# Asking for the half-heads 2 and 3 of the linear attention at four steps per product instead of two

## The chip, the cores and the metric

The kernel runs on one core of a Trainium2 chip. The metric is the time of one launch on the device, in microseconds. Beside the times there is a profile of one execution, which shows what each engine did when. TensorE is called PE in it, VectorE DVE, ScalarE ACT, GpSimd POOL, and SyncE, which issues most DMAs, SP.

## The reference

The kernel computes two layers of a streaming-encoder trunk on 512 tokens of width 2048, in float32. Each layer normalises its input, projects it to 7184 columns, and splits them between a gated linear attention (GLA, four heads, called half-heads here since they make one half of the output's input) and a chunked attention of eight heads. Each group is normalised per head, gated and concatenated; one output projection, a second normalisation and the residual follow.

```python
z = h @ w_in
gq, gk, gv, gg, ga, aq, ak, av, ag = split_columns(z)
...
U = jnp.einsum('bnchk,bnchv->bnhkv', k_dec, vf)
...
new = a[..., None] * state + u
...
o = jnp.einsum('bnchk,bnhkv->bnchv', qf, states)
...
o_gla = rmsnorm(o_gla, g_gla.reshape(GLA_HEADS, GLA_DV)).reshape(B, S, D_GLA)
o_gla = o_gla * jax.nn.silu(gg)
...
y = jnp.concatenate([o_gla, o_att], axis=-1) @ w_out
return x + rmsnorm(y, g_post)
```

The recurrence goes over eight chunks of 64 tokens: U is the outer product of a chunk's decayed keys and its values, the state is decayed and U added, and the chunk's queries read the new state.

## The kernel before

The projections are done in blocks of 512 columns. Float32 products are made of three matmuls on a high and a low part of each operand: `wh` is the weight's rounded copy (ACT, L203), `wl` the rest (DVE, L207). Some blocks are plain (`std_gemm`, matmuls at L323): for each of eight 256-row chunks of the contraction, four token tiles with six matmuls each. Others go in pairs (`fast_gemm`, L409 and L399) with a Strassen-like scheme of seven products (P1, P5, P6, P3, P7, P2, P4) of four chunks each; one chunk of a product is twelve matmuls of 128x512. A list called `stream` fixes the order of all weight blocks, and `ahead` loads and splits them a few entries in advance.

Between these matmuls the small work of the two attentions is woven in. It is written as Python generators in a list `tasks`; one advance of the first generator is a step. After each matmul group `Pace` calls `pump` with so many steps as its `rate` says; `delayed` holds work that comes due a number of steps later. The finished program is then put in order by the framework's scheduler, which places each engine's instructions by what it reckons to be ready.

The last pair of a layer's input blocks is the value pair, `PAIRS[5]`. Its products P3 and P7 finish the values of half-heads 2 and 3 (`j` = 1 in `gv_consume`), and P2 and P4 those of half-heads 0 and 1. When the second token half of a `j` is there, `gv_consume` appends `gla_heads(j, ...)` to `tasks`: for `j` = 1 alone, for `j` = 0 beside `early_sums`, of which one step is taken for every third of the heads. `gla_heads` works on four units, one for each half-head and each token half p. A unit's steps are:

- `outer` (PE, L1060): twelve matmuls with 64 contraction rows, two groups of six that go to the two PSUM tiles `ps_u[0]` and `ps_u[1]`, for even and odd chunks.
- `states` (SP loads the gate, L1069; DVE, L1079 and L1081): four dependent updates of the state.
- `read` (PE, L1094): four matmuls that read the states into `ps_o`.
- `norm` (ACT, L1104 and L451; POOL's power, L447).
- `gate` (DVE, L1112), which leaves the gated output in a buffer `bias` or `sg`, used in turn.
- `turn`, five steps later (PE transposes, L1122; ACT, L1133; POOL stores it, L1137; ACT and DVE split it, L108 and L109), which makes an operand of the output projection.

The names `bias` and `sg` in L1122's rows are those buffers, `a120` to `a123` and `g4`, `g5`, `g16`, `g17` the operands that the turns make. The small PSUM tiles (`ax`) come from a pool of four buffers.

Next in `stream` is the first output block, `std_gemm(l, NB_IN, ...)` at a rate of 1.7 steps per six matmuls. Its chunks come in the order `OO`, the GLA half-heads last, in the order 2, 3, 0, 1. Behind it `until(lambda: len(og) == 8)` takes what steps the turns still need, the eight loads of x are issued on POOL behind the last norm (L479), and the second block begins with `NB_IN + 1` and two of four token tiles. `early_sums` and `output_sums` load the attention outputs back (SP, L637 for `fa`, L641 for `fg`), form sums and differences of them (DVE, L604, split by L108 and L109) and store them (POOL, L611), for the last pair of the output projection.

Of the kernel before, what the change touches and what calls it, by code (L numbers as in the profile page):

```python
# [34 lines left out]
def hybrid_trunk(  # L35
# [92 lines left out]
    PAIRS = ((GG0, GG1), (AV0, AV1), (QK01, QK23), (QK45, QK67), (GK, GQ), (GV0, GV1))  # L128
# [558 lines left out]
    def layer(l):  # L687
# [520 lines left out]
                tasks.append(heads if j else beside(heads, early_sums(), 3))  # L1208


        fast_gemm(l, PAIRS[5], gv_consume, rate=2, after=fetch_operands)
        A.clear()


# [113 lines left out]
    for l in range(L):  # L1328
        layer(l)
# [54 lines left out]
```

## Time and profile before

| what | value |
|---|---|
| median of three runs | 1643.76 us (1642.11 to 1644.25) |
| the profiled execution | 1642.16 us, span 1640.4 us |
| instructions | 24886 |
| busy PE, DVE, ACT, POOL | 1623.6, 1227.6, 905.5, 178.2 us |
| DMA, mean over the span | 286 GB/s |

The span is the time from the first to the last instruction; the execution's own time has 1.8 us more around it. A row of the timeline gives the start, the duration, the engine, the line and the operation, the tile written and those read, the shape, and the count of instructions that were merged; square brackets hold the idle time just before it and what ended that. Matmuls overlap, so the pitch of a stream of them is read from the difference of their starts. In a row of the waits stand the waiting engine and line, what it waited for, the total, the count and the longest.

### The profile page before, as it was taken

Reading aid. Unit: us, or ns where it says so; the run is one execution under the profiler, and the core shown is the slowest. Engines: PE = TensorE matmul, PEld = TensorE weight load, DVE = VectorE, ACT = ScalarE, POOL = GpSimd, SP = SyncE. Lnnn points to the kernel's source line nnn. Section 1 sums busy time; section 2 is a strip of 40 time slices with the busy share of each in tenths; the row PEclk is TensorE's granted clock in tenths of the full one; section 3 lists DMA queues with packets and bytes.
Section 4 is the critical chain, followed back from the end, with each engine's and each line's share of the span. In section 5 each row is a group of like instructions: output and inputs, shape, how many; then the busy total and the mean of one; then the engine's idle time right before and its main releaser. Section 6 shows DMA issues by size and latency. Waiting matters only on the chain.

```text
span 1640.4 us, 24886 instructions
## 1 busy us (share of the span) xinstructions
PE 1623.6 (99%) x9030; PEld 1392.1 (85%) x9030; DVE 1227.6 (75%) x1579; ACT 905.5 (55%) x1515; POOL 178.2 (11%) x259
## 2 busy tenths in 40 slices
PE   9999999999999999999999999999999999999997
PEld 7888889999988877688888888899999888776886
DVE  7567776877877876678776676768778778857887
ACT  7444544556666644455784445445556765445553
POOL 1210000001101201310132000000001001013111
PEclk9999999999999999999999999999999999999999
DMA  9979796958858696899779797968588676967996
GB/s 380 350 273 320 281 313 228 309 173 309 293 179 297 206 383 211 283 370 357 285 257 383 267 338 258 322 220 302 192 310 271 207 271 232 357 230 287 394 327 226
DMA packets 150490, 469.59 MB, mean 286 GB/s; under 512 B 16396, under 2 KB 35604, under 8 KB 150368
## 3 DMA queue, kind: packets, MB, share of 16 engines
q1 hardware_dynamic: 127632, 389.36, 68.3%
q0 software_dynamic: 22016, 77.37, 12.1%
q8 instruction: 71, 1.16, 0.3%
q10 hardware_dynamic: 720, 1.28, 0.2%
q14 instruction: 51, 0.42, 0.1%
HBM read 395.83 MB, written 71.06 MB: 285 GB/s over the span
## 4 chain that ended last, share of the span: by engine, by line
PE 97%; DVE 1%; DMA 1%; ACT 1%; issue 0%; DVEq 0%; POOL 0%; SPq 0%; ACTq 0%; POOLq 0%
PE mm L409 45%; PE mm L323 21%; PE mm L399 20%; PE ax L890 2%; PE ax L409 1%; PE ax L873 1%; PE ax L1060 1%; PE ax L721 1%; PE ax L1094 1%; PE ax L853 1%; PE ax L852 1%; PE ax L851 1%; DMA t<-fg 0%; PE ax L921 0%; PE ax L551 0%
## 5 line engine op out<-in xcount | busy, mean ns | idle before, releaser
L409 PE MATMUL mm<-wh,sa 128*128 128x512 f32 x1536 | 484.6, 391 | 0.1
L203 ACT CAST wh<-raw 128x1024 fp32r<-128x1024 f32 x256 | 270.1, 1056 | 262.9 <-PE mm L409 113.3
L207 DVE TENSOR_TENSOR wl<-raw,wh 128x1024 fp32r<-128x1024 f32 x256 | 312.6, 1222 | 122.6 <-PE mm L323 39.0
L203 ACT CAST wh<-H 128x1024 fp32r<-128x1024 f32 x224 | 235.5, 1053 | 221.4 <-PE mm L409 115.1
L207 DVE TENSOR_TENSOR wl<-H,wh 128x1024 fp32r<-128x1024 f32 x224 | 273.8, 1223 | 109.0 <-PE mm L409 50.4
L409 PEld LDWEIGHTS mm<-wh,sa 128*128 128x128 f32 x1536 | 288.0, 188 | 62.3 <-issue 2.4
L409 PE MATMUL mm<-wl,sa 128*128 128x512 f32 x768 | 300.3, 391 | 0.1
L399 PE MATMUL mm<-sa,wh 128*128 128x256 f32 x1280 | 237.1, 285 | 0.0
L399 PEld LDWEIGHTS mm<-sa,wh 128*128 128x128 f32 x1280 | 199.9, 191 | 0.3
L409 PE MATMUL mm<-wh,a 128*128 128x512 f32 x576 | 186.3, 393 | 0.0
L399 PE MATMUL mm<-sa,wl 128*128 128x256 f32 x640 | 180.6, 283 | 0.0
L323 PE MATMUL mm<-wh,a 128*128 128x512 f32 x512 | 167.9, 394 | 4.0 <-ACT a L108 1.2
L409 PEld LDWEIGHTS mm<-wl,sa 128*128 128x128 f32 x768 | 144.2, 188 | 29.6 <-DVE wl L207 0.5
L447 POOL TENSOR_TENSOR sm<-sm,mhalf 128x4 f32<-128x4 f32 (+2 forms) x40 | 67.1, 1678 | 767.1 <-DVE sm L906 542.0
L197 DVE TENSOR_TENSOR H<-H,raw 128x1024 f32<-128x1024 f32 x120 | 146.5, 1221 | 1.7
L409 PEld LDWEIGHTS mm<-wh,a 128*128 128x128 f32 x576 | 108.0, 188 | 22.5
L399 PEld LDWEIGHTS mm<-sa,wl 128*128 128x128 f32 x640 | 122.3, 191 | 0.1
L323 PEld LDWEIGHTS mm<-wh,a 128*128 128x128 f32 x512 | 96.0, 188 | 27.5 <-DVE g L1242 2.0
L409 PE MATMUL mm<-wl,a 128*128 128x512 f32 x288 | 112.9, 392 | 0.0
L323 PE MATMUL mm<-wl,a 128*128 128x512 f32 x256 | 100.4, 392 | 0.5 <-DVE wl L207 0.5
L399 PE MATMUL mm<-a,wh 128*128 128x256 f32 x512 | 94.7, 285 | 0.0
L323 PE MATMUL mm<-wh,sa 128*128 128x512 f32 x256 | 87.0, 396 | 0.0
(203 smaller groups left out, 2324.8 us busy)
## 6 DMA issues: line engine op xcount, KB each, us to landing
raw<-in_w_dram SPq DMA_DIRECT2D x320, 512.0 KB, 5.6
sa<-S SPq DMA_DIRECT2D x192, 512.0 KB, 4.7
H<-in_w_dram SPq DMA_DIRECT2D x56, 512.0 KB, 4.7
sa<-A SPq DMA_DIRECT2D x48, 512.0 KB, 6.5
S<-g POOLq DMA_DIRECT2D x32, 512.0 KB, 7.7
oS<-g POOLq DMA_DIRECT2D x32, 512.0 KB, 6.3
sa<-oS SPq DMA_DIRECT2D x32, 512.0 KB, 5.5
sg<-t POOLq DMA_DIRECT2D x32, 256.0 KB, 5.7
```

The lines of the kernel that those rows point to most:

```text
L197: nc.vector.tensor_tensor(out=h, in0=h, in1=r, op=ALU.add)
L203: last_cast[0] = nc.scalar.copy(self.wh, src).ins
L207: last_low[0] = nc.vector.tensor_tensor(out=self.wl, in0=self.src, in1=self.wh.bitcast(F32), op=ALU.subtract).ins
L323: mm = nc.tensor.matmul(pss[o], a[:, part, t], rhs[:, kk, :], start=(i == 0 and kk == 0 and m == 0), stop=(i == n - 1 and kk == 1 and m == 2),
L399: nc.tensor.matmul(dst, lhs[:, kk, f], a[:, part, tok], start=(fresh and kk == 0 and m == 0 and ft % 2 == 0), stop=(c == c_last and kk == ...
L409: nc.tensor.matmul(out_ps[t], a[:, part, tok], rhs[:, kk, :], start=(fresh and kk == 0 and m == 0), stop=(c == c_last and kk == 1 and m == ...
L447: return nc.gpsimd.tensor_tensor(out=out_r, in0=v, in1=mhalf[:, : v.shape[-1]], op=ALU.pow).ins
L721: nc.tensor.matmul(ps[0:96, half * 256 : (half + 1) * 256], wga[kt // 10][:, kt % 10, :], op[:, i, (kt % 2) * 256 : (kt % 2 + 1) * 256], s ...
L851: nc.tensor.matmul(ps[:, :n], self.qh[:, t], self.kh[:, :n], start=True, stop=False)
L852: nc.tensor.matmul(ps[:, :n], self.qh[:, t], self.kl[:, :n], start=False, stop=False)
L853: nc.tensor.matmul(ps[:, :n], self.ql[:, t], self.kh[:, :n], start=False, stop=True)
L890: nc.tensor.matmul(o, self.pt[i][:, j * P : (j + 1) * P], av[hd // 4, j // 2][:, j % 2, (hd % 4) * P : (hd % 4 + 1) * P], start=(j == 0), ...
```

## The change

The pace in the value pair is four steps per chunk of a product instead of two.

```diff
-        fast_gemm(l, PAIRS[5], gv_consume, rate=2, after=fetch_operands)
+        fast_gemm(l, PAIRS[5], gv_consume, rate=4, after=fetch_operands)
```

Up to the last chunks of P2 the order of every engine is as before: no step waits in `tasks` there. From then on half-heads 2 and 3 come earlier, and with them everything that follows them in `tasks`. Each layer changes in the same way. The rows below are from layer 0, with the number of each tile.

On PE, the outer products of the second unit of half-head 3, before (in the first output block; `ax_1230` and `ax_1231` are the unit's two PSUM tiles):

```order
L323 MATMUL mm_1226_6462<-wh_1189_6329,a111_1150_6131 128x512
L1060 MATMUL ax_1230_6480<-g5_1160_6177,g11_1027_5565 128x256
L1060 MATMUL ax_1231_6481<-g5_1160_6177,g11_1027_5565 128x256
L1060 MATMUL ax_1230_6480<-g7_1161_6178,g11_1027_5565 128x256
L1060 MATMUL ax_1231_6481<-g7_1161_6178,g11_1027_5565 128x256
L1060 MATMUL ax_1230_6480<-g5_1160_6177,g15_1029_5567 128x256
L1060 MATMUL ax_1231_6481<-g5_1160_6177,g15_1029_5567 128x256
```

The other six follow in the same alternation, and then L323. The same unit after, now within P4 (`ax_1211` and `ax_1212` are the two tiles):

```order
L1060 MATMUL ax_1211_6396<-g5_1160_6177,g11_1027_5565 128x256
L1060 MATMUL ax_1211_6396<-g7_1161_6178,g11_1027_5565 128x256
L1060 MATMUL ax_1211_6396<-g5_1160_6177,g15_1029_5567 128x256
L409 MATMUL mm_1065_5718<-wh_1184_6292,sa_1175_6256 128x512
L409 MATMUL mm_1065_5718<-wl_1190_6330,sa_1175_6256 128x512
L409 MATMUL mm_1065_5718<-wh_1184_6292,sa_1175_6256 128x512
L1060 MATMUL ax_1212_6397<-g5_1160_6177,g11_1027_5565 128x256
L1060 MATMUL ax_1212_6397<-g7_1161_6178,g11_1027_5565 128x256
L1060 MATMUL ax_1212_6397<-g5_1160_6177,g15_1029_5567 128x256
```

Each tile's six matmuls (the three rows twice) now stand together, with block matmuls between the two sixes. Half-head 3's first unit, half-head 0's second and half-head 1's first stand in this way too; before, only half-head 0's second did.

On PE, the last two turns and what follows them in the first output block, before (`bias` and `sg` are the gated outputs, `a121` the operand made by the first of the two turns):

```order
L323 MATMUL mm_1228_6464<-wh_1258_6630,g4_1315_6903 128x512
L1122 MATMUL ax_1336_6987<-cst_203,bias_1291_6795 128x128 x4
L1122 MATMUL ax_1346_7030<-cst_203,sg_1312_6887 128x128 x4
L323 MATMUL mm_1225_6461<-wh_1283_6741,a121_1337_6992 128x512
L323 MATMUL mm_1225_6461<-wl_1301_6833,a121_1337_6992 128x512
```

and after:

```order
L1122 MATMUL ax_1327_6903<-cst_203,bias_1285_6717 128x128
L323 MATMUL mm_1248_6541<-wl_1318_6877,a120_1287_6734 128x512
L1122 MATMUL ax_1327_6903<-cst_203,bias_1285_6717 128x128 x3
L323 MATMUL mm_1248_6541<-wh_1303_6800,a120_1287_6734 128x512 x2
L323 MATMUL mm_1248_6541<-wl_1318_6877,a120_1287_6734 128x512
L323 MATMUL mm_1248_6541<-wh_1303_6800,a120_1287_6734 128x512
L1122 MATMUL ax_1334_6946<-cst_203,sg_1306_6809 128x128
L323 MATMUL mm_1249_6542<-wh_1303_6800,g4_1309_6831 128x512
L1122 MATMUL ax_1334_6946<-cst_203,sg_1306_6809 128x128 x3
L323 MATMUL mm_1249_6542<-wl_1318_6877,g4_1309_6831 128x512
```

The turns now stand within the chunk before, that of half-head 0, and the rest of that chunk lies between them and the first reader of `a121`.

On DVE, the first sum of the output operands (L604) and the state updates of half-head 0's second unit around it (`g10_1271` before, `g10_1262` after). Before:

```order
L1081 SCALAR_TENSOR_TENSOR g10_1271_6681<-g9_1263_6646,a_end_13_247,ax_1272_6682 128x256
L604 TENSOR_TENSOR t2_1270_6670<-t2_1269_6669,t2_1270_6670 128x512
L1081 SCALAR_TENSOR_TENSOR g10_1271_6681<-g10_1271_6681,a_end_13_247,ax_1273_6683 128x256
L1081 SCALAR_TENSOR_TENSOR g10_1271_6681<-g10_1271_6681,a_end_13_247,ax_1272_6682 128x256
L604 TENSOR_TENSOR t2_1269_6669<-t2_1267_6667,t2_1269_6669 128x512
```

and after:

```order
L1081 SCALAR_TENSOR_TENSOR g10_1262_6597<-g9_1254_6562,a_end_13_247,ax_1263_6598 128x256
L207 TENSOR_TENSOR wl_1281_6706<-raw_1242_6528,wh_1268_6636 128x1024
L604 TENSOR_TENSOR t2_1261_6592<-t2_1260_6591,t2_1261_6592 128x512
L1081 SCALAR_TENSOR_TENSOR g10_1262_6597<-g10_1262_6597,a_end_13_247,ax_1264_6599 128x256
L1081 SCALAR_TENSOR_TENSOR g10_1262_6597<-g10_1262_6597,a_end_13_247,ax_1263_6598 128x256
```

The neighbourhood is the same but for the low part of a weight ahead of the sum; on PE the same updates are read after other matmuls than before.

## The prediction

> **What bounds the kernel now.** I read the page first: which engine is busy and what the chain that ended last is made of.
>
> ```profile
> span 1640.4 us, 24886 instructions
> PE 1623.6 (99%) x9030; PEld 1392.1 (85%) x9030; DVE 1227.6 (75%) x1579; ACT 905.5 (55%) x1515; POOL 178.2 (11%) x259
> PE 97%; DVE 1%; DMA 1%; ACT 1%; issue 0%; DVEq 0%; POOL 0%; SPq 0%; ACTq 0%; POOLq 0%
> ```
>
> TensorE is the bound: 97% of the chain. A change can gain in two ways only, by removing time in which PE waits, or by making PE's own instructions cheaper. So next came PE's waits, and then the stages in which they fall.
>
> ```profile
> PE ax L1122 <- issue: 2.2, 2, 1.1
> PE mm L323 <- ACT a L108: 1.2, 2, 0.6
> PE mm L323 <- DVE g L1242: 1.2, 2, 0.6
> ```
>
> ```profile
> 583.00:632.00 49.00, 48.93 (x238) 37.33 (x238) 39.75 (x49) 22.43 (x30) 0.71 (x1) 1.00 0.90 335
> 632.00:675.00 43.00, 43.00 (x239) 31.66 (x238) 26.32 (x46) 20.46 (x51) 8.24 (x12) 1.00 0.60 204
> 675.00:720.00 45.00, 42.64 (x197) 33.23 (x196) 29.91 (x41) 23.75 (x45) 12.48 (x22) 1.00 0.98 364
> 720.00:795.00 75.00, 75.00 (x332) 62.09 (x331) 69.63 (x76) 40.76 (x58) 11.53 (x14) 1.00 0.94 351
> 1490.00:1535.00 45.00, 42.34 (x195) 32.83 (x194) 29.51 (x42) 22.47 (x45) 13.16 (x23) 1.00 0.97 362
> ```
>
> (Columns of the stretches: length; busy PE, weight loads, DVE, ACT, POOL; granted clock, DMA share, GB/s.) The value pair ends near 632 and the first output block near 693; layer 1 repeats this 815 us later. PE is full in the pair and in most of the block, and idles only at the block's end: 2.36 us in layer 0, 2.66 in layer 1. The clock is 1.00 throughout and plays no part. PE's timeline shows the place, layer 0 first:
>
> ```profile
> 686.74 0.60 PE L1122 MATMUL ax<-cst,bias 128*128 128x128 f32 x4
> 688.43 0.90 PE L1122 MATMUL ax<-cst,sg 128*128 128x128 f32 x4 [1.09 <-issue]
> 689.95 0.50 PE L323 MATMUL mm<-wh,a 128*128 128x512 f32 x1 [0.62 <-ACT a L108]
> ...
> 692.57 0.39 PE L323 MATMUL mm<-wh,a 128*128 128x512 f32 x1
> 693.56 0.50 PE L323 MATMUL mm<-wh,a 128*128 128x512 f32 x1 [0.60 <-DVE g L1242]
> ```
>
> ```profile
> 1497.80 1.08 PE L1094 MATMUL ax<-g,g 128*64 128x256 f32 x8
> 1499.19 0.50 PE L323 MATMUL mm<-wh,g 128*128 128x512 f32 x1 [0.31 <-ACT g L108]
> ...
> 1502.09 0.60 PE L1122 MATMUL ax<-cst,bias 128*128 128x128 f32 x4
> ...
> 1505.29 0.50 PE L323 MATMUL mm<-wh,a 128*128 128x512 f32 x1 [0.62 <-ACT a L108]
> ...
> 1507.92 0.39 PE L323 MATMUL mm<-wh,a 128*128 128x512 f32 x1
> 1508.91 0.50 PE L323 MATMUL mm<-wh,a 128*128 128x512 f32 x1 [0.60 <-DVE g L1242]
> ```
>
> The turns (L1122) of the last two units stand bare in front of the last chunk that needs them: PE has nothing left to put between. An undisturbed turn is this:
>
> ```profile
> 641.37 0.60 PE L1122 MATMUL ax<-cst,sg 128*128 128x128 f32 x4
> 641.73 0.48 PE L323 MATMUL mm<-wl,a 128*128 128x512 f32 x1
> ```
>
> **The change part by part. First, the bare tail goes.** Twice as many steps per product finish half-heads 2 and 3 inside the pair, so 0 and 1 start earlier, and in the new order the last two turns have 40 and 35 matmuls of their block behind them, of which 16 and 23 stand before the first that reads what they make (3.7 and 5.3 us at the pitch of 0.23). Layer 0: 686.74 to 689.95 is 3.21 us for two turns that cost 0.36 each undisturbed, so 2.49 too much; the later gap, 692.57 to 693.56, is 0.99 where the pitch is 0.23, so 0.76. Sum 3.25. Layer 1: 3.20 - 0.72 = 2.48, the same 0.76, and 0.31 of the wait at 1499.19: 3.55. Gain 6.8 us in both.
>
> **Second, the outer products get dearer.** L1060 issues twelve matmuls per unit with 64 contraction rows each: six for the even chunk into one PSUM tile, six for the odd one into another. Before, seven of eight units alternate between the two. In the new order four units (both of half-head 3, the second of half-head 0, the first of half-head 1) are cut into six for one tile, some block matmuls, six for the other; before, one was. The one unit that is cut already gives the price. A whole alternating unit, then the first half of the cut one, as stretches (L1060 alone) and in the timeline:
>
> ```profile
> 613.02:613.97 0.95, 0.90 (x12) 0.77 (x12) 1.00 1.03 405
> 655.90:656.84 0.94, 0.90 (x6) 0.76 (x6) 1.00 0.83 232
> ```
>
> ```profile
> 612.75 0.39 PE L409 MATMUL mm<-wh,a 128*128 128x512 f32 x1
> 613.07 0.97 PE L1060 MATMUL ax<-g,g 64*128 64x256 f32 x12
> 613.97 0.50 PE L409 MATMUL mm<-wh,a 128*128 128x512 f32 x1
> 614.31 0.40 PE L409 MATMUL mm<-wl,a 128*128 128x512 f32 x1
> ```
>
> ```profile
> 655.63 0.39 PE L323 MATMUL mm<-wh,a 128*128 128x512 f32 x1
> 655.95 0.97 PE L1060 MATMUL ax<-g,g 64*128 64x256 f32 x6
> 656.84 0.50 PE L323 MATMUL mm<-wh,a 128*128 128x512 f32 x1
> ```
>
> Twelve alternating take 0.90 us, and six for one tile take 0.90 too: the two row halves run beside each other only when they alternate. Matmul to matmul, the alternating unit adds 1.22 - 0.23 = 0.99, each half 1.21 - 0.23 = 0.98. Cutting a unit costs 0.97, or 1.08 with the slower pitch behind a run (0.34 for 0.23). Three more cut units: 2.9 to 3.2, taken 3.1. Besides, one unit is cut two and ten, one goes four, four and then alternating, one read (L1094) is cut three and one: each 0.1 to 0.4 by a run's ends (0.09 before it, 0.11 behind) and a few unpaired matmuls of 0.15, together 0.4 to 1.1, taken 0.7. Against that, six runs now touch another small run instead of standing alone; if a shared edge saves the 0.2 of two ends, that is 1.2, if none, 0. No row here has L1060 next to L1094, so I take 0.4. Per layer 3.1 + 0.7 - 0.4 = 3.4, bounds 2.1 and 4.3; for both layers 6.8, bounds 4.2 and 8.6.
>
> [...]
>
> **Third, what is moved past what.** On DVE the pair takes in four more state updates, a gating multiply and half a split before 632. State updates are 0.50 each (1.51 for three, below), the 128x512 pieces 0.69: some 3.7 us into a stretch where DVE was busy 39.75 of 49. The cover is DVE's 9 idle us; the low parts (L207) that PE needs are made as soon as one of three buffers is free, at least one product (2.7 us) ahead. ACT has 27 idle us there. On SP the gate loads (L1069), the fa and fg loads and the gain row go some 10 us earlier past the weight loads, which run four buffers ahead. POOL's norm power comes earlier, and with it the eight loads of x behind the last norm: they stay in the stretch of 364 GB/s, but begin while the block is still running. I cost all three at nothing.
>
> The closest place is the first sum of the output operands (L604), which waits on DVE for a load and has three state updates behind it:
>
> ```profile
> 652.92 0.60 PE L1122 MATMUL ax<-cst,sg 128*128 128x128 f32 x4
> 656.05 0.56 SPq L641 DMA_DIRECT2D t<-fg  x1
> 661.18 0.69 DVE L604 TENSOR_TENSOR t<-t,t 128x512 f32<-128x512 f32 x1 [3.39 <-DMA t<-fg]
> 661.78 1.51 DVE L1081 SCALAR_TENSOR_TENSOR g<-g,a_end,ax 128x256 f32<-128x256 f32 x3
> ```
>
> ```profile
> 1470.97 0.56 SPq L641 DMA_DIRECT2D t<-fg  x1
> 1476.75 0.69 DVE L604 TENSOR_TENSOR t<-t,t 128x512 f32<-128x512 f32 x1 [4.00 <-DMA t<-fg]
> DMA to landing us min/median/max: 4.2/5.7/11.5
> ```
>
> The turn at 652.92 frees the gate buffer, SP gets to the loads, and the updates end 10.4 us after the turn (663.29). In the new order PE needs them 28 block matmuls (6.4), the turn (0.36), a unit (0.99), two half units (2.0), a read (1.39 - 0.31 = 1.1, at 1497.80) and a half unit (1.0) later: 11.8. The margin is 1.4 us in layer 0; the load took 5.1 us there and 5.8 in layer 1, so 0.7 there.
>
> **Sum.** -6.8 + 6.8 = 0, bounds -2.6 and +1.8, against the profiled execution's 1642.16 us (span 1640.4 and 1.8 around it). The median of the runs shown is 1643.76, 1.6 higher, and the new median moves with it: I forecast 1643.8, with 1641 to 1646 as this case's own range.
>
> **The rivals.** *A load holds PE (slower).* L604 waits longer than before, the state updates behind it are late, and PE waits at a half unit or read in both layers. It decides once a load takes over 6.5 us (5.1 + 1.4) from issue to landing. The median is 5.7, the maximum 11.5; the gain row's load now sits just ahead of these four. At 8 to 9 us it costs 1.5 to 2.5 per layer, at 11.5 us 5.0: 1647 to 1654, typically 1648. Against it: no PE wait follows from L604 today, and the DMA share is 0.60 in that stretch.
>
> *The tail wait survives (slower).* The second group of fa and fg loads comes to lie behind the first load of a finished sum on SP; if these sums reach DVE late, the last turns are bare again. The cuts are paid and nothing is gained: 1643.8 + 6.8 = 1650.6. Against it: the last turns stand 35 matmuls, 8 us, before the block's end.
>
> *The cuts cost little (faster).* If the cut halves cost only their ends (0.2 for each of three units instead of 1.0), the layer pays 0.9 rather than 3.4: 1643.8 - 5.0 = 1638.8. For it: PE could have waited for a buffer within the one cut unit shown. Against it: both halves of that unit have the same length in both layers.
>
> That the change does nothing is excluded: the order on all five queues differs from the pair's last products on.
>
> **How the numbers follow.** A measurement of this kernel can tell 0.2%, 3.3 us, from no change. No change 0.62, a late load 0.16, the tail wait survives 0.08, cheap cuts 0.14. So faster 0.14, same 0.62, slower 0.24. For 8 in 10 the range reaches from 1640 into the typical late load, to 1649.
>
> **What would show it.** Right: no bare pair of L1122 in front of an L323 with a wait for L108; eight stretches of six L1060 per layer with 0.90 us each; PE's idle time smaller by about 5 us and its busy time larger by as much; L604 still waiting 3 to 4 us without a PE wait near it. Wrong: PE waits at L1060 or L1094 for DVE (the late load), L1122 still waiting (the tail), or a cut half of about 0.5 us (cheap cuts).

## The result and the profile after

The changed kernel takes 1654.41 us (median of six runs, 1650.43 to 1655.91), the kernel before beside it 1643.83 (1642.11 to 1644.63): ratio 1.0058, 95% interval 1.0049 to 1.0068. It is slower by 10.6 us, and 1643.8 with a range to 1649 was forecast. From here on the page of the changed kernel, then its waits of PE:

```profile
span 1653.1 us, 24894 instructions
PE 1635.3 (99%) x9030; PEld 1401.7 (85%) x9030; DVE 1228.0 (74%) x1579; ACT 904.3 (55%) x1515; POOL 172.1 (10%) x259
PE 97%; DMA 2%; DVE 1%; ACT 0%; issue 0%; DVEq 0%; POOL 0%; SPq 0%; POOLq 0%
```

```profile
PE mm L323 <- ACT wh L203: 5.1, 3, 2.3
PE mm L323 <- DVE wl L207: 2.3, 3, 0.9
```

The waits of the bare tail (L1122, and L323 for L108 and L1242) are gone as forecast, and waits for the weights' two parts stand there in their place. Of each, one of the three lies at the kernel's start (1.0 and 0.5 us, 0.8 and 0.5 before). The other two lie in the second output block:

```profile
717.27 0.73 PE L323 MATMUL mm<-wh,a 128*128 128x512 f32 x2 [2.28 <-ACT wh L203]
718.90 0.79 PE L323 MATMUL mm<-wl,a 128*128 128x512 f32 x1 [0.89 <-DVE wl L207]
...
720.34 0.63 PE L323 MATMUL mm<-wl,a 128*128 128x512 f32 x1
720.77 0.63 PE L323 MATMUL mm<-wh,a 128*128 128x512 f32 x1
...
1537.18 0.77 PE L323 MATMUL mm<-wh,a 128*128 128x512 f32 x2 [1.82 <-ACT wh L203]
1538.82 0.79 PE L323 MATMUL mm<-wl,a 128*128 128x512 f32 x1 [0.87 <-DVE wl L207]
```

Behind the two pauses the pitch is 0.43 (720.34 to 720.77) instead of 0.23: the granted clock falls, as the stretches show (columns as in the prediction).

```profile
705.00:715.00 10.00, 10.00 (x45) 7.94 (x43) 1.75 (x3) 0.44 (x1) 0.55 (x1) 1.00 1.03 387
715.00:720.00 5.00, 1.84 (x5) 1.21 (x6) 4.93 (x8) 4.36 (x6) 0.54 (x1) 0.85 1.04 399
720.00:725.00 5.00, 5.00 (x20) 4.03 (x19) 4.66 (x6) 2.82 (x5) 1.12 (x3) 0.80 1.03 411
1535.00:1540.00 5.00, 2.31 (x7) 1.29 (x6) 4.93 (x8) 4.43 (x6) 0.54 (x1) 0.77 1.03 396
1540.00:1545.00 5.00, 5.00 (x14) 3.87 (x13) 4.67 (x5) 2.68 (x4) 1.07 (x2) 0.54 1.04 415
```

From 705 to 715 DVE is busy for 1.75 of 10 us and ACT for 0.44: both wait, while the DMA is full. What they wait for stands in their timelines (SP's issues first, then DVE and ACT):

```profile
695.80 0.53 SPq L637 DMA_DIRECT2D t<-fa  x1
696.71 0.33 SPq L641 DMA_DIRECT2D t<-fg  x1
698.52 0.53 SPq L637 DMA_DIRECT2D t<-fa  x1
700.38 0.33 SPq L641 DMA_DIRECT2D t<-fg  x1
700.79 0.38 SPq L154 DMA_DIRECT2D raw<-in_w_dram  x1
```

```profile
706.71 1.23 DVE L207 TENSOR_TENSOR wl<-raw,wh 128x1024 fp32r<-128x1024 f32 x1 [1.27 <-PE mm L323]
714.91 1.42 DVE L604 TENSOR_TENSOR t<-t,t 128x512 f32<-128x512 f32 x2 [6.98 <-DMA t<-fg]
...
717.63 1.22 DVE L207 TENSOR_TENSOR wl<-raw,wh 128x1024 fp32r<-128x1024 f32 x1
```

```profile
715.64 0.62 ACT L108 CAST g<-t 128x512 fp32r<-128x512 f32 x1 [10.20 <-DVE t L604]
716.17 1.04 ACT L203 CAST wh<-raw 128x1024 fp32r<-128x1024 f32 x1
```

The second load of `fg` for the sums of chunk 0 is issued at 700.38 and lands 14.4 us later. On DVE the sum (L604) waits for it, and the next low part (717.63) comes behind the sum. ACT's cast of that sum (L108) waits 10.2 us with the next `wh` behind it. The next weight load (700.79) stands behind four loads of sums as well, and takes as long (the DMA view of 700.3 to 700.8: size, us from issue to landing):

```profile
raw<-in_w_dram SPq DMA_DIRECT2D x1, 512.0 KB, 15.3
t<-fg SPq DMA_DIRECT2D x1, 256.0 KB, 14.4
```

So these weights are there at 716.1, and the cast that makes their `wh` begins at 716.17. In layer 1 it is 1535.9 and 1536.09. The cast of the sum (L108) ends about when the weights come: without it ahead, the cast of the weights could have begun 0.1 and 0.2 us earlier and no more. In the kernel before the same stretch reads so (SP, DVE, ACT):

```profile
699.27 1.71 SPq L154 DMA_DIRECT2D raw<-in_w_dram  x2
...
701.56 0.53 SPq L637 DMA_DIRECT2D t<-fa  x1
...
703.47 0.58 SPq L641 DMA_DIRECT2D t<-fg  x1
```

```profile
711.02 1.23 DVE L207 TENSOR_TENSOR wl<-raw,wh 128x1024 fp32r<-128x1024 f32 x1 [1.76 <-ACT wh L203]
...
716.63 1.41 DVE L604 TENSOR_TENSOR t<-t,t 128x512 f32<-128x512 f32 x2
```

```profile
709.93 1.05 ACT L203 CAST wh<-raw 128x1024 fp32r<-128x1024 f32 x1 [1.94 <-DMA raw<-in_w_dram]
```

There the block's last two weight loads are issued ahead of the loads for the sums (the second of them takes 9.2 us to land in layer 1), and its last raw low part (711.02) stands ahead of the first sum (716.63), which waits for nothing.

To place the loss, each layer is cut at starts read from the timelines: the first L1060, ACT's fourth row of L1239, and the first L409 of the last pair. "Block 1" and "block 2" lie between these. Each evacuation of a token tile has two rows of L1239, so the fourth row belongs to the second of the first block's four tiles, not to the last evacuation, as the expectations below call it. How much of the work lies ahead of it depends on the order: 180 L323 in the kernel before, 184 in the changed one, and four are 0.9 us at the pitch of 0.23. "Both" therefore goes on to the third L409 of the last pair; ahead of that, the same matmuls lie in every run. "Rest" goes from there to the next layer's first L1060 or the end.

| profiled execution | to the first L1060 | block 1, layer 0 / 1 | block 2, layer 0 / 1 | both, layer 0 / 1 | rest, layer 0 / 1 |
|---|---|---|---|---|---|
| before | 596.93 | 96.56 / 96.94 | 22.42 / 22.42 | 121.70 / 122.08 | 693.27 / 106.41 |
| after | 598.63 | 97.86 / 97.77 | 26.68 / 27.25 | 127.26 / 128.01 | 693.19 / 106.04 |

The spans differ by 12.7. Of that 1.7 lies ahead of the change's first effect (the profiled executions of the kernels below scatter from 596.8 to 598.8 there), 11.5 in the two blocks, and -0.5 in the rest. With four matmuls taken off, the first block is longer by 0.4 and -0.1: nearly all of the loss lies in the second.

### The profile page after: what moved, and what is told of

It reads as the page before. It is cut to its first block, busy times and chain, and to the rows that moved or that the text cites. A ratio compares the mean times of both kernels' runs of the same rounds, so it can differ in the third digit from the quotient of the medians.

```text
span 1653.1 us, 24894 instructions
## 1 busy us (share of the span) xinstructions
PE 1635.3 (99%) x9030; PEld 1401.7 (85%) x9030; DVE 1228.0 (74%) x1579; ACT 904.3 (55%) x1515; POOL 172.1 (10%) x259
## 4 chain that ended last, share of the span: by engine, by line
PE 97%; DMA 2%; DVE 1%; ACT 0%; issue 0%; DVEq 0%; POOL 0%; SPq 0%; POOLq 0%
PE mm L409 45%; PE mm L323 20%; PE mm L399 19%; PE ax L890 2%; DMA t<-fg 2%; PE ax L1060 1%; PE ax L409 1%; PE ax L873 1%; PE ax L1094 1%; PE ax L721 1%; PE ax L853 1%; PE ax L852 1%; PE ax L851 1%; PE ax L1122 0%; PE ax L921 0%; PE ax L551 0%
## 5 line engine op out<-in xcount | busy, mean ns | idle before, releaser
L409 PE MATMUL mm<-wh,sa 128*128 128x512 f32 x1536 | 484.4, 391 | 0.1
L409 PEld LDWEIGHTS mm<-wh,sa 128*128 128x128 f32 x1536 | 288.0, 188 | 61.5 <-issue 2.2
L409 PE MATMUL mm<-wl,sa 128*128 128x512 f32 x768 | 300.3, 391 | 0.0
L409 PE MATMUL mm<-wh,a 128*128 128x512 f32 x576 | 186.9, 394 | 0.0
L323 PE MATMUL mm<-wh,a 128*128 128x512 f32 x512 | 170.6, 401 | 5.9 <-ACT wh L203 5.1
L409 PEld LDWEIGHTS mm<-wl,sa 128*128 128x128 f32 x768 | 144.3, 188 | 29.3
L447 POOL TENSOR_TENSOR sm<-sm,mhalf 128x4 f32<-128x4 f32 (+2 forms) x40 | 60.9, 1524 | 768.9 <-DVE sm L906 542.9
L409 PEld LDWEIGHTS mm<-wh,a 128*128 128x128 f32 x576 | 108.2, 188 | 23.2 <-issue 0.8
L323 PEld LDWEIGHTS mm<-wh,a 128*128 128x128 f32 x512 | 97.8, 192 | 28.6 <-ACT wh L203 6.7
L409 PE MATMUL mm<-wl,a 128*128 128x512 f32 x288 | 113.4, 394 | 0.0
L323 PE MATMUL mm<-wl,a 128*128 128x512 f32 x256 | 102.9, 402 | 2.3 <-DVE wl L207 2.3
L108 ACT CAST g<-t 128x512 fp32r<-128x512 f32 (+3 forms) x116 | 57.6, 531 | 57.5 <-DVE t L604 36.6
```

Of the source, the lines that this page charges most:

```text
L108: nc.scalar.copy(hi, src)
L323: mm = nc.tensor.matmul(pss[o], a[:, part, t], rhs[:, kk, :], start=(i == 0 and kk == 0 and m == 0), stop=(i == n - 1 and kk == 1 and m == 2),
L409: nc.tensor.matmul(out_ps[t], a[:, part, tok], rhs[:, kk, :], start=(fresh and kk == 0 and m == 0), stop=(c == c_last and kk == 1 and m == ...
L447: return nc.gpsimd.tensor_tensor(out=out_r, in0=v, in1=mhalf[:, : v.shape[-1]], op=ALU.pow).ins
```

## The experiments

Theories at the start: *late load* (an `fg` load behind the `x` loads holds up the low parts on DVE) and, as its rival, *cut outer products* (they cost far more than the rows said). A third came with the first results: *SP's wait* for a finished sum. All results, with the stages as above; the last column is the time over that of the kernel before. Ahead of the mark between the blocks lie 188 L323 in e4, e9 and e12, 180 and 182 in e11, and 184 in the others; block 2 of e1 and e11, and of e4 in layer 0, has ten more of them at its end than the others. Where it matters, compare "both".

| run | median, us | block 1 | block 2 | both | rest | ratio, 95% |
|---|---|---|---|---|---|---|
| e1 | 1658.65 | 97.80 / 98.10 | 27.42 / 30.57 | 125.67 / 129.12 | 695.71 / 107.60 | 1.0096 (1.0083 to 1.0109) |
| e2 | 1654.58 | 97.79 / 98.43 | 21.52 / 21.52 | 122.03 / 122.67 | 699.62 / 109.77 | 1.0060 (1.0046 to 1.0073) |
| e3 | 1644.28 | 95.78 / 95.79 | 24.06 / 24.03 | 122.56 / 122.54 | 693.59 / 106.04 | 1.0000 (0.9991 to 1.0008) |
| e4 | 1657.56 | 101.24 / 102.85 | 25.09 / 23.32 | 126.79 / 128.89 | 693.94 / 106.60 | 1.0083 (1.0070 to 1.0096) |
| e5 | 1652.46 | 97.85 / 97.92 | 25.83 / 24.38 | 126.40 / 125.02 | 693.75 / 105.98 | 1.0054 (1.0040 to 1.0068) |
| e6 | 1643.12 | 95.78 / 95.79 | 24.58 / 23.41 | 123.08 / 121.92 | 693.51 / 105.98 | 0.9998 (0.9989 to 1.0006) |
| e7 | 1648.93 | 97.99 / 98.21 | 21.52 / 21.52 | 122.23 / 122.45 | 695.90 / 109.31 | 1.0029 (1.0017 to 1.0040) |
| e8 | 1644.97 | 95.79 / 95.79 | 21.52 / 21.52 | 120.03 / 120.03 | 696.47 / 108.51 | 1.0008 (0.9999 to 1.0017) |
| e9 | 1644.08 | 98.66 / 98.66 | 22.01 / 20.80 | 123.39 / 122.18 | 693.76 / 106.22 | 1.0003 (0.9994 to 1.0012) |
| e10 | 1645.10 | 95.78 / 95.79 | 24.52 / 22.22 | 123.02 / 120.73 | 694.87 / 107.52 | 1.0006 (0.9997 to 1.0015) |
| e11 | 1643.99 | 96.61 / 98.32 | 24.67 / 24.16 | 121.73 / 122.93 | 695.27 / 106.44 | 0.9999 (0.9990 to 1.0008) |
| e12 | 1648.11 | 98.66 / 98.66 | 20.62 / 20.61 | 122.00 / 121.99 | 694.22 / 107.96 | 1.0029 (1.0020 to 1.0038) |
| e13 | 1655.51 | 97.80 / 98.91 | 28.21 / 24.62 | 128.77 / 126.25 | 694.14 / 106.53 | 1.0070 (1.0058 to 1.0082) |
| e14 | 1652.11 | 96.72 / 96.73 | 26.98 / 25.86 | 126.46 / 125.33 | 694.53 / 106.62 | 1.0055 (1.0042 to 1.0068) |
| e15 | 1651.55 | 95.79 / 95.79 | 21.52 / 21.52 | 120.03 / 120.03 | 699.43 / 111.82 | 1.0052 (1.0040 to 1.0064) |
| e16 | 1643.90 | 97.80 / 98.48 | 21.52 / 21.52 | 122.04 / 122.72 | 693.01 / 105.97 | 1.0003 (0.9994 to 1.0012) |
| e17 | 1639.74 | 95.79 / 95.79 | 21.52 / 21.52 | 120.03 / 120.03 | 693.00 / 105.98 | 0.9976 (0.9967 to 0.9985) |

Where a run adds lines, the L numbers in its rows below lie one or two above those of the changed kernel.

**e1: x later.**

```diff
-                nc.gpsimd.dma_start(of_gla[l][p, h], full_o)
+                last_put[0] = nc.gpsimd.dma_start(of_gla[l][p, h], full_o).ins
...
-        with tc.issue_after(last_norm[0]):
+        with tc.issue_after(last_put[0]):
             xs0 = load_tokens(0, x_src, nc.gpsimd)
```

> The changed kernel, with its loads of x (L479) put on POOL behind the last two stores of fg instead of ahead of them; outer products, rates and the place of the sums on DVE as in the changed kernel. Late load (the fg load of the sums for chunk 0 takes 14 us beside the x loads, and L604 holds up the low parts behind it on DVE): the load lands in under 8 us, no wait of L323 for L203 or L207 over 0.5 us near 717 and 1537, and the 5.1 + 5.9 us of the two stalls go: about 1643.5, between 1641 and 1647. Cut outer products: all cuts stand, so 1654 as the changed kernel. DMA simply full (the same bytes before the same point): the load is as late as before, 1652 to 1655.

A miss for the first two. The `x` loads moved only from 7.3 to about 4 us ahead of the mark, and the load lands as late:

```profile
713.33 1.42 DVE L605 TENSOR_TENSOR t<-t,t 128x512 f32<-128x512 f32 x2 [6.15 <-DMA t<-fg]
```

That is the mechanism of the third expectation (the same bytes ahead of the same point), but 1658.65 lies above its 1652 to 1655: the waits in the second block stay (3.1 and 3.6 us), and PE waits 1.3 us in each last pair besides, where the changed kernel doesn't wait.

**e2: sums behind all low parts of the block.**

```diff
-        std_gemm(l, NB_IN + 1, (0, 1), ..., rate=0.6, lag=2)
+        std_gemm(l, NB_IN + 1, (0, 1), ..., rate=0.6, skip=12, lag=2)
```

> The changed kernel, with no step taken in the first twelve groups of the second output block, so that the sums of chunks 0 and 1 (L604) come behind all low parts of that block on DVE; PE's order up to there is that of the changed kernel, cuts included. Late load: no L323 waits for L203 or L207 in the second block; 1654.4 - 11.0 = 1643.4, up to 1647 if the later sums now hold up the first product of the last pair that reads them. Cut outer products: 1654. If the later sums only carry the wait into the last pair: 1650 to 1655 with PE waits at L409.

The second block runs without a wait, 21.52 in both layers with all cuts in it: the stall doesn't need the cuts to go. But the loads are issued later too, and the last pair waits for the finished sum:

```profile
753.98 0.47 PE L409 MATMUL mm<-wh,sa 128*128 128x512 f32 x1 [3.95 <-DMA sa<-oS]
```

**e3: no cuts.**

```diff
+                prev = None
...
-                            nc.tensor.matmul(self.ps_u[cc][...], ...)
+                            with tc.issue_after(prev) if prev else nullcontext():
+                                prev = nc.tensor.matmul(self.ps_u[cc][...], ...).ins
```

> The changed kernel, with each matmul of an outer product issued behind the one before it, so that even and odd chunks alternate again (one matmul alone, then eleven in alternation, in each unit); the sums in the second output block stand as in the changed kernel. Late load: the wait for L203 and L207 in the second block stays at 3 us per layer; the four cut units per layer get cheaper by 0.97 each, less up to 0.3 per unit for the unpaired matmul and its ends: 1654.4 - 3 to -7, so 1647.5 to 1651.5. Cut outer products as the cause of the loss: 1643.8 or less, and no stall worth naming.

By the time this is the rival's result, all of the loss gone. By the stages it isn't: the first block is 2.0 us shorter per layer, 4.1 in all, and the second falls from 26.68 and 27.25 to 24.1, with pauses of 2.0 and 1.9 us still in it. Why they are shorter without the cuts isn't shown. Behind these the clock stays at 1.00:

```profile
712.21 0.73 PE L323 MATMUL mm<-wh,a 128*128 128x512 f32 x2 [1.08 <-ACT wh L203]
713.82 0.50 PE L323 MATMUL mm<-wl,a 128*128 128x512 f32 x1 [0.88 <-DVE wl L207]
```

**e4: the kernel before with early sums.** `rate=1.7` of the first output block becomes 2.2.

> The kernel before (value pair at two steps), with the first output block at 2.2 steps per group instead of 1.7: the early sums are done sooner, and the sums of chunks 0 and 1 come to stand on DVE ahead of four low parts of the second block, nearly as in the changed kernel. Late load: L323 waits 2 to 3 us for L203 or L207 in the second block of each layer without the value pair's change; with the clock behind it 4 to 6 us per layer, and two more cut units (1.9 per layer): 1651 to 1656. Cut outer products: no wait there; two more cut units of the three that the change adds, so two thirds of its 10.6 us: 1650.9, by the 0.97 of a cut alone 1647.7.

The stall appears without the change: L323 waits near 718 and 1540, 1.6 and 2.1 us per layer, less than the 2 to 3 expected in layer 0. The first block's tail stays bare (2.2 us for L108 in each layer, where the kernel before idles 2.4 and 2.7 in all). "Both" is longer by 5.1 and 6.8 us. The rest of that has several parts that this run doesn't separate: two more cut units, and in layer 1 a granted clock of 0.87 and 0.79 in the stretches 1513 to 1518 and 1518 to 1523, behind the tail's wait. The median lies 1.6 us above the expected range.

```profile
718.15 0.73 PE L323 MATMUL mm<-wh,a 128*128 128x512 f32 x2 [0.51 <-ACT wh L203]
720.00 0.50 PE L323 MATMUL mm<-wl,a 128*128 128x512 f32 x1 [1.11 <-DVE wl L207]
```

**e5 and e6: sums held back, loads early.** Four more steps between chunk 0's loads and its sums, and the sums placed behind the last low part so far:

```diff
+            for _ in range(4 if end and c == 0 else 0):
+                yield
...
-            with tc.issue_after(last_state[0]) if end else nullcontext():
+            gate = last_low[0] if chunks == (0, 1) else last_state[0]
+            with tc.issue_after(gate) if end else nullcontext():
```

> The changed kernel, with the sums of chunks 0 and 1 (L604) held back behind the low parts on DVE, while the loads of chunk 0 (fa, fg) are issued at the same place as in the changed kernel; the loads of chunk 1 come later. Outer products as in the changed kernel. Late load: no L323 waits for L203 or L207 in the second block; from the end of the first block's last evacuation to the first matmul of the last pair 22.4 us as before the change, not 26.7 and 27.2: 1654.4 - 4.3 - 4.8 = 1645.3, up to 1650 if the late chunk 1 now holds up the last pair (L409 waits for sa). Cut outer products alone: 1654.

> The run above with alternating outer products as well. If the two causes add up: e3_no_cuts (1644.3) less its remaining stalls of 1.6 per layer: 1641.0, faster than the kernel before by 3; between 1639 and 1645 if the late chunk 1 costs something in the last pair. If the cuts were the only cause: 1644.

A miss that taught most. The sums are out of the way on DVE, and PE still waits, 2.4 and 2.2 us. A weight load is late itself (SP, then ACT):

```profile
699.92 18.93 SPq L154 DMA_DIRECT2D raw<-in_w_dram  x6
```

```profile
714.92 1.04 ACT L203 CAST wh<-raw 128x1024 fp32r<-128x1024 f32 x1 [10.36 <-DMA raw<-in_w_dram]
```

It lands 15.0 us after its issue, behind four loads of sums and the `x` loads, as the same load did in the changed kernel (15.3). So the order on SP is enough for the stall; that on DVE adds 0.8 and 0.5 us of pauses (3.2 and 2.7 in the changed kernel). e6, the same without cuts, has a stall of nearly the same size (24.6 and 23.4) and a first block shorter by 2.1 per layer. That and the stalls' difference make 6.4; the medians differ by 9.3, so 3 us of it aren't in these two executions (1650.79 and 1645.35).

**e7 and e8: x behind the stores of the sums.** The two lines that load `x` stand behind the second block's `std_gemm`, with `tc.issue_after` the last store of a sum (L611).

> The changed kernel, with the loads of x behind the eight stores of the sums (L611) on POOL, so that 4 MB less lie ahead of the fg loads; cuts as in the changed kernel, sums on DVE as early or earlier. Late load under a full DMA: the fg load lands in 4 to 8 us instead of 14, no wait of L323 in the second block, about 1645, up to 1648 if x now comes late for the end of the layer. DVE order alone, without the load (DVE simply has too much to do there): the stall stays, 1652 to 1656.

> The run above with alternating outer products as well. If the causes add up: 1645 - 4.1 = 1641, between 1639 and 1644. If the cuts do all: 1644 and the same stall as in e3_no_cuts, 2 us per layer.

With 4 MB less ahead of them the loads are in time: 21.52 in all four blocks. The last pair gets longer instead (rest 695.9 and 109.3, against 693.2 and 106.0 in the changed kernel), and PE waits there (the waits of e7):

```profile
PE mm L410 <- DVE wl L207: 2.1, 4, 0.5
PE mm L410 <- ACT wh L203: 1.8, 2, 1.4
```

e8 is 4.0 us faster than e7 in the median, with first blocks shorter by 2.2 and 2.4: the cuts' price once more.

**e9 to e12: finished sums behind the weights on SP.** In the changed kernel SP waited 10.4 us at the load of a finished sum, with three weight loads behind it.

```diff
-                nc.sync.dma_start(flat(self.a), src)
+                with tc.issue_after(last_load[0]) if end else nullcontext():
+                    nc.sync.dma_start(flat(self.a), src)
```

> The changed kernel, with the loads of the finished sums (sa, L187) put on SP behind the weight loads that the program issued before them, so that SP no longer waits up to 10 us for an sa buffer with three weight loads of the second block behind it. Cuts, sums on DVE and loads of x as in the changed kernel. SP's wait as the cause: the weights (L154) of the second block are issued before 686 instead of up to 694, the DMA no longer falls to 160 GB/s about 13 us before the block and moves some 0.6 to 1.2 MB more ahead of it, 1.5 to 3 us of each of the two stalls go: 1648 to 1651. The late load behind the x loads as the whole cause: the fg load is issued where it was and lands as late, 1653 to 1655.

> The run above with alternating outer products: if the causes add up, 4.1 less than the run above, 1644 to 1647 less up to 3: about 1641.5 where e3_no_cuts gave 1644.3, and its stalls of 2 us per layer smaller by half or more. If SP's wait plays no part: 1644.3.

> The kernel before with the same order on SP. It has no stall in the second block to lose: 1643.8 by each theory, between 1642.5 and 1645; slower only if the sums then come too late for the last pair.

> e5_sums_held (sums of chunks 0 and 1 behind the low parts, 1652.5, in which ACT waited 10 us for a weight load) with the sa loads behind the weights too; cuts as in the changed kernel. If the stall is the DMA's backlog, which the weights now miss: no wait for L203 or L207 in the second block, 21.5 us there instead of 25.8 and 24.4, and 1652.5 - 4.3 - 2.9 = 1645.3, up to 1650 if the last pair then waits for its sums. If the cuts alone were the cause: 1652.

e9 loses nothing against the kernel before, more than its theory gave. That looked like the cause. But taking out the cuts gains nothing on top: in e10 PE waits 2.4 and 0.4 us in the second block, in e9 0.8 and none, and the rest is 1.1 and 1.3 us longer. e12 pays in the last pair (rest 1.0 and 1.9 us longer than in the changed kernel). e11 is unchanged in the median, as each theory said.

**e13: only the load that SP waited on.** As e9, for the second such load of each layer alone.

> The changed kernel, with only the second load of a finished sum in each layer (the sa load that SP waited on for 10 us) put behind the weight loads; the first stands where it stood, PE's order up to the end of the first block is the changed kernel's, cuts and tail included. If SP's wait there is the cause: as e9, 1643.5 to 1646, the second block at 22.5 us or less in place of 26.7 and 27.2. If the sa loads of the last pair made e9's gain: 1651 to 1655.

SP's wait as the cause falls: 1655.51. The weights go out without that wait, and the block stalls as before:

```profile
716.88 1.22 PE L325 MATMUL mm<-wh,a 128*128 128x512 f32 x2 [3.15 <-ACT wh L205]
```

e9 differs by the other loads it moved; its `x` loads also begin 9.0 us ahead of the same matmul instead of 7.3 (687.38 and 697.31, less 0.9 for four matmuls, against 689.16 and 696.49), and the weight load behind the four loads of sums takes 13.0 us instead of 15.3 (16.2 in e13). Which of these saved it was not tried by itself.

**e14: three steps.** `rate=3` for the value pair.

> The kernel before with three steps per product instead of two or four. The sums of chunks 0 and 1 stand on DVE where the changed kernel has them, ahead of the low parts, and the x loads ahead of their fg load; one unit and parts of two more are cut; but on SP one weight load more stands ahead of the sa load that waits. SP's wait: a stall as in e3_no_cuts, 1.6 us per layer, and about 1.5 for cuts: 1644 to 1648. Late load behind early sums on DVE: 5 us per layer, 1652 to 1655.

1652.11, on the side of the late load: the loss doesn't go with the number of cuts (one unit is cut in sixes, as in the kernel before, and parts of others; block 1 at 96.7), but with the order in the second block, which is nearly that of the changed kernel. There the weight load behind the sums takes 14.5 us.

**e15: e10 with x behind the sums' stores.**

> e10 (sa behind the weights, no cuts, 1645.1) with the x loads behind the stores of the sums. If the full DMA ahead of the second block is what gives back the gain of the uncut outer products: the second block at 21.5 us in both layers, and 1641, as long as x out there does not hold up the last pair; in e8 it cost about 3 us per layer there, by which this run too would end at 1644 to 1646: then the DMA sets the pace of the whole stretch, wherever x stands.

Worse than both ends of the expectation: block 2 is clean and the last pair loses 6 us per layer. The wait is moved, not removed.

**e16 and e17: the old order in the second block.** Both orders that e4, e14 and the changed kernel share are undone without making the sums late: the loads of chunks 0 and 1 go behind the last weight load issued so far, their sums behind the last low part (as in e5), and the block starts its steps four groups later at 0.9 instead of 0.6.

```diff
+                with tc.issue_after(last_load[0]) if chunks == (0, 1) else nullcontext():
                     nc.sync.dma_start(tiles[2 * half]..., of_att[l][c]...)
                     nc.sync.dma_start(tiles[2 * half + 1], of_gla[l][half, c])
...
-        std_gemm(l, NB_IN + 1, (0, 1), ..., rate=0.6, lag=2)
+        std_gemm(l, NB_IN + 1, (0, 1), ..., rate=0.9, skip=4, lag=2)
```

> The changed kernel, with the order of the kernel before restored in the second output block alone: on SP the last two weight loads of the block stand ahead of the loads of the chunk 0 sums again, on DVE the block's low parts stand ahead of these sums. First block, cuts, tail and x loads as in the changed kernel. If these two orders are the cause: no L323 waits near 717 and 1537, 21.5 to 22.5 us from the last evacuation to the last pair in place of 26.7 and 27.2, and nothing given back in the last pair: 1654.4 - 9.5 = 1645, between 1643 and 1647. If a full DMA moves the wait on wherever the loads stand: waits at L409 in the last pair and 1649 to 1655, as in e2.

> The run above with alternating outer products. If cuts and the new order add up: 1645 - 4.1 = 1641, faster than the kernel before by 0.1 to 0.2%. If the DMA takes back what PE gains ahead of the second block, as between e9 and e10: 1644 to 1645.

Both as expected by the first of their theories. In e16 (SP, ACT, DVE):

```profile
698.63 4.00 SPq L154 DMA_DIRECT2D raw<-in_w_dram  x2
702.67 0.53 SPq L639 DMA_DIRECT2D t<-fa  x1
...
704.66 0.57 SPq L643 DMA_DIRECT2D t<-fg  x1
```

```profile
710.88 1.05 ACT L203 CAST wh<-raw 128x1024 fp32r<-128x1024 f32 x1 [3.94 <-DMA raw<-in_w_dram]
```

```profile
711.96 1.23 DVE L207 TENSOR_TENSOR wl<-raw,wh 128x1024 fp32r<-128x1024 f32 x1 [3.11 <-ACT wh L203]
...
715.63 1.42 DVE L605 TENSOR_TENSOR t<-t,t 128x512 f32<-128x512 f32 x2 [1.31 <-DMA t<-fg]
```

The `fg` load lands at 715.6, later than in the changed kernel, and it doesn't matter: the last weights are there by 710.9 (the second load is issued at 702.3 and takes 8.5 us), and their low part (711.96) is done ahead of the sum. No wait of L323 is left in the block, and the last pair pays nothing (rest 693.0 and 106.0). All cuts are still in; the whole loss is gone. e17 without cuts is 4.2 us faster again, 1639.74, below both kernels.

## Why the prediction was wrong

**The step that failed** is the third, "what is moved past what": "I cost all three at nothing". It held two mistakes. SP was said to run four weight buffers ahead, so that loads moved past weights cost nothing; in the second block the last two weight loads came to stand behind the four loads of sums, and the first of them took 15.3 us to land under the `x` traffic, where the later of the two took 9.2 before. The cast that PE waited for began 0.1 and 0.2 us after that landing. And only the first sum of the output operands was examined, at 661 us, where a margin was worked out; the sums of chunks 0 and 1 in the second block also came earlier, ahead of the low parts on DVE and the casts on ACT, where the load of `fg` takes 14.4 us. Restoring both orders takes 1654.4 to 1643.9 (e16). Restoring DVE's alone gives 1652.5 (e5), which leaves most of the loss with SP's; no run restores SP's alone.

The row to read was in hand: the stretch from 675 to 720 had a DMA share of 0.98, and the rival "a load holds PE" had the right kind of mechanism, a late load, though it meant the load of a sum and not of a weight. It was put at the wrong place (half units and reads in block 1, in the stretch with a share of 0.60) and priced at 1.5 to 2.5 us per layer, 5.0 at most, with 0.16. At that place nothing came of it: the first sum waits 2.5 and 3.4 us for its load in the changed kernel, and no wait of PE follows. The new block 2 is 5.2 and 5.7 us longer than the 21.52 without a stall (e16, the same order on PE), of which the pauses are 3.2 and 2.7; the other 2.0 and 3.0 come with the slow clock behind them (0.80 from 720 to 725, 0.54 from 1540 to 1545), which the prediction called "plays no part".

**First, the tail.** Right in kind: the last two turns have block matmuls between them and no bare wait. **Second, the cuts.** A cut half is 0.90 as forecast:

```profile
661.85 0.97 PE L1060 MATMUL ax<-g,g 64*128 64x256 f32 x6
662.75 1.08 PE L1094 MATMUL ax<-g,g 128*64 128x256 f32 x8
663.77 0.50 PE L323 MATMUL mm<-wl,sa 128*128 128x512 f32 x1
```

The six matmuls and the read behind them take 0.90 and 1.02 from start to start, with nothing between: the ends of 0.11 and 0.09 that each run has against a block matmul are missing there. So a shared edge does save 0.2. The forecast took 0.4 per layer for six such edges, a third of six times 0.2.

The balance of the two terms came out nearly as forecast: +0.15 and -0.15 us per layer forecast, and +0.34 and +0.64 measured from the kernel before to e16 ("both", the same matmuls; 0.26 of the 0.64 is a wait ahead of a turn). e16's ratio of 1.0003 is the "no change" that was forecast. How the balance divides isn't shown. The tail's 3.25 and 3.55 were taken from gaps between starts, while PE had idled 2.36 and 2.66; if only these idle times were gained, the dearer instructions cost 2.7 and 3.0 instead of 3.4, and both terms were too large, by 0.9 and by 0.7 and 0.4. That they still balance would then be luck in part. Four cut units against none (e16 and e17) are 2.0 and 2.7 us per layer; e17's units still stand as one and eleven, which costs something too: from start to start one alone takes 0.31 (at 659.29) and eleven 0.91 (at 655.55), where an alternating twelve took 0.90 in the kernel before.

**The rivals.** "The cuts cost little" and "the tail wait survives" did not come.

## What to carry to other kernels

Where the DMA is full, the order of loads in a queue is a term of the sum (in layer 1 here a weight load behind four loads of sums took 14.7 us to land, and 9.2 ahead of them in the kernel before): list for every moved step which loads now stand ahead of the data that the bound engine needs next, and do it for each later stage that the step's followers reach, not only for the first. Where an instruction stands waiting for a load, ask what the bound engine needs from behind it, and then whether that had its own data yet: the sum on DVE looked like the cause, and the weights behind it weren't there either. Taking a wait away at one place of a full stretch often only moves it (e2, e7, e15); a table of stage lengths shows that at once, where the total alone misleads (e3 seemed to prove the rival, e9 a third theory). The stages must hold the same work in every run, or the mark itself makes a difference (0.9 us here).

## What the runs showed of the hardware

A pause of PE can cost more than itself. After pauses of 2.28 and 0.89 us within 4 us the pitch went from 0.23 to 0.43; after 1.82 and 0.87 in layer 1 the granted clock in a stretch of 5 us fell to 0.54. It is not certain: after 1.08 and 0.88 (e3) it stayed at 1.00, and after 1.64 and 1.42 in layer 0 of e1 too. The same pause can go both ways: behind 2.24 at the tail in layer 0 of e4 it stayed at 1.00, and behind 2.23 in its layer 1 the pitch was 0.43 (1517.03 to 1517.45) and the clock 0.87 and 0.79 in two stretches of 5 us. Nor does the length tell: 1.00 and 0.53 in the last pair of e15's layer 0 were followed by a pitch of 0.43 and a clock of 0.82 and 0.83, the 1.97 and 0.53 in layer 0 of e6 by 1.00. What decides isn't shown.

Loads under a full DMA took 14.4 us (`fg`, 256 KB) and 15.3 us (weights, 512 KB) to land, at 387 to 415 GB/s and a share of 1.03 to 1.04; in the stretch with a share of 0.60 the kernel before had 5.1 us for `fg` (656.05 to 661.18).
